# Three reorderings in a two-layer decoder trunk: a mean ahead of its root, sines behind two casts, and one store in place of two

## The chip, the cores and the metric

The kernel runs on 1 core of one Trainium2 chip. The metric is the device time of one execution in microseconds (us); the median of three runs stands for a kernel. TensorE (PE) multiplies matrices and loads weights (PEld), VectorE (DVE), ScalarE (ACT) and GpSimd (POOL) do the elementwise work, SyncE (SP) issues most of the DMAs.

## The reference

256 tokens of 1024 features pass through two layers. All is float32.

```
h = rmsnorm(x, norm_mix);  cb, cc, cu, q, k, v, g, ga, gb = split(h @ w_in)
y_conv = (cb * short_conv(cc * cu)) @ w_conv_out
q, k = rotary(q), rotary(k)              # sines and cosines of positions * frequencies
o = retention(q, k, v)                   # 4 heads, decay masks, two chunks of 128
o = (o - mean) * rsqrt(var + EPS) * ret_norm;   y_ret = (silu(g) * o) @ w_ret_out
x = x + (sigmoid(ga) * y_conv + sigmoid(gb) * y_ret) @ w_o
x = x + square(relu(rmsnorm(x, norm_mlp) @ w_up)) @ w_down
```

After the second layer the output is `rmsnorm(x, norm_final)`.

## The kernel before

The residual stream lies in SBUF with features on partitions and tokens along the free dimension. Weights come from HBM in 152 blocks of 1 MB, each as two half-blocks of 512 KB. For precision each half-block is split into a high and a low part: ACT casts it (`split`, L105), DVE subtracts the high part (L106). TensorE works on the parts, some 24 or 32 matmuls a block.

One call of `window` is one block. It writes out, in a fixed order, what each engine's queue gets: work at phase -1, then phase 0, the split of the first half of the block after next, phase 1, the split of the second half, phase 2, and the matmuls of its own block. Blocks 4 and 5 take the first split ahead of phase 0. `at(n, fn, ph=p)` puts a function into the window n blocks on; `products_at` does it for small matmuls. The schedule is manual: each engine runs its queue in this order and waits where a semaphore tells it to.

`rsqrt_begin` (L244) starts a reciprocal square root: ACT looks up a first value y (L246), DVE makes the mean m (L247); both read the same sums v in PSUM. `newton` then refines y: a square on ACT (L240), two multiplies on DVE (L241, L242). `rsqrt_begin` is called in `factors_begin` (once a layer, for the first norm, with Newton steps in the next two windows) and in `head_roots` (twice a layer, for the variances of two heads each, with Newton steps two and three windows on). Between `head_roots` and what follows on ACT's queue stand the collect of a projection (`collect`, L234 on ACT, L235 on DVE) and the two casts.

In layer 0 POOL reduces the rotary angles; `sines` (L389) takes two sines and an absolute value on ACT; `rotation_tables` (L395) makes the two tables with four POOL instructions; `rotations` (L422) multiplies the tables by the norm's factor on DVE, in window 8. ACT must load a table of functions (ACT_TABLE_LOAD) before it can take a sine, a root or a tanh.

At the end the last block's products are squared and summed for each of two halves of 128 tokens; `root(1)` gives the factor r. The last 512 features of the second half are scaled on DVE by `scaled` (L813) in two pieces of 256, each stored by a DMA that SP issues; the first 512 are scaled on ACT and stored from ACT's queue.

Of the kernel before, what the change touches and what calls it, by code (L numbers as in the profile page):

```python
# [16 lines left out]
ALU = mybir.AluOpType  # L17
# [8 lines left out]
EPS = 1e-6  # L26
# [27 lines left out]
def trunk_kernel(ctx, tc, px, pos, w, mask, gf, out):  # L54
    nc = tc.nc
# [31 lines left out]
    class Parts:  # L87
# [5 lines left out]
        def at(self, k):  # L93
            return self.tiles[k // (KT // 2)][:, k % (KT // 2)]
# [148 lines left out]

    def rsqrt_begin(y, m, v, scale):  # L244

        nc.scalar.activation(y, v, AF.Abs_reciprocal_sqrt, scale=scale, bias=eps)  # L246
        nc.vector.tensor_scalar(out=m, in0=v, scalar1=scale, scalar2=EPS, op0=ALU.mult, op1=ALU.add)  # L247

    def column_sums(o, hi, lo):

# [87 lines left out]
    for n in range(2):  # L338
        c = slice(4 * n, 4 * n + 4)
# [9 lines left out]
    def first_parts(norm=norm):  # L349

        def parts(i, *ks):
            for n, k in enumerate(ks):
                norm.split(k)
                split_half(i, n)

        at(0, parts, 1, 2, 3)
        at(1, parts, 2, 4, 5)
        at(2, parts, 3, 6, 7)
        at(3, norm.split, 0)
        for i, half in ((4, 0), (4, 1)):  # L360
            at(3, split_half, i, half)
        for p in range(NPAIR):
            at(3 if p < 3 else 4, norm.square, p)
        at(4, norm.fold)
        at(5, norm.split_sum)
# [37 lines left out]
    for layer in range(DEPTH):  # L403
# [4 lines left out]
        def factors_begin(norm=norm):  # L408
            rs_m, rs_a = (tmp.tile([P, T], F32, tag="tmp1", bufs=7, name=n) for n in ("rs_m", "rs_a"))
            rsqrt_begin(rr, rs_m, norm.total_ps, 1.0 / D)  # L410
            at(1, newton, rr, rs_a, rs_m, ph=-1)
            at(2, factors_end, rs_m, rs_a, ph=-1)
# [17 lines left out]
        if layer == 0:  # L430
            first_parts()
            at(0, reduce_angles)
            at(5, sines, ph=2)
            at(6, rotation_tables)
            at(9, nc.sync.dma_start, mask_sb, mask)
        if layer == 0:
            products_at(5, norm_total)
# [144 lines left out]
        def head_roots(i, st):  # L582

            if i == 0:
                new("rm", s8.tile([P, 2, HEADS, T], F32, tag="s8", name="rm"))
            rm = kept["rm"]
            h = slice(2 * i, 2 * i + 2)
            rs = rm[:, 0, h, :]
            rsqrt_begin(rs, rm[:, 1, h, :], st, 1.0 / T)
            later = 2 + i  # L590
            for n in range(2):
                at(later + n, lambda: newton(rs, t2("rs_a"), rm[:, 1, h, :]))
            for n in range(2):
                at(later + 1 + n, head_out, 2 * i + n, rs[:, n, :])
# [17 lines left out]
        for name, _ in IN_ORDER:  # L612
            n = seen[name] = seen.get(name, -1) + 1
# [183 lines left out]
    def root(j):  # L797

        rest, part = sums[j][:, 0:1], sums[j][:, 1:2]
        m, r, a = (small.tile([P, 1], F32, tag=f"{n}{j}", bufs=1, name=n) for n in ("fin_m", "fin_r", "fin_a"))  # L800
        nc.scalar.activation(r, part, AF.Sqrt, bias=rest)
        nc.vector.tensor_tensor(out=m, in0=part, in1=rest, op=ALU.add)
        nc.vector.reciprocal(r, r)
        nc.vector.scalar_tensor_tensor(out=a, in0=r, scalar=m, in1=r, op0=ALU.mult, op1=ALU.mult)
        nc.vector.scalar_tensor_tensor(out=r, in0=a, scalar=3.0, in1=r, op0=ALU.subtract, op1=ALU.mult)
        return r
# [6 lines left out]
    def scaled(j, n, c, r):  # L813

        f = slice(512 * n + c.start, 512 * n + c.stop)
        nc.vector.scalar_tensor_tensor(
            out=o[j][:, f], in0=ps[j][n][:, c], scalar=r, in1=gain[:, f], op0=ALU.mult, op1=ALU.mult
        )
        nc.sync.dma_start(out=out[tok[j], f], in_=o[j][:, f])
# [19 lines left out]
    c = HALVES[0]  # L839
# [2 lines left out]
    nc.vector.tensor_tensor(out=o[1][:, c], in0=ps[1][0], in1=gain[:, c], op=ALU.mult)  # L842
    squares(1, 1)
    r = root(1)
    for n in range(2):
        scaled(1, 1, slice(256 * n, 256 * n + 256), r)
    nc.scalar.activation(o[1][:, c], o[1][:, c], AF.Copy, scale=r)
    nc.scalar.dma_start(out=out[tok[1], c], in_=o[1][:, c])

# [73 lines left out]
```

## Time and profile before

| | |
|---|---|
| median of 3 runs | 876.67 us (876.5 to 876.76) |
| the profiled execution | 876.84 us |
| its span in the profile | 875.0 us |
| PE busy | 866.8 us (99%) |
| DVE, ACT, POOL busy | 680.2, 529.5, 308.4 us |
| mean granted TensorE clock | 0.999 of full speed |

The span runs from the first to the last instruction that the profiler recorded; the execution's own time has a little more around it. Busy TensorE time is modelled from pipelined matmuls, so that a short starvation shows better in the waits than in the busy share.

### The profile page before, as it was taken

Reading aid. Unit: us, or ns where it says so; the run is one execution under the profiler, and the core shown is the slowest. Engines: PE = TensorE matmul, PEld = TensorE weight load, DVE = VectorE, ACT = ScalarE, POOL = GpSimd, SP = SyncE. Lnnn points to the kernel's source line nnn. Section 1 sums busy time; section 2 is a strip of 40 time slices with the busy share of each in tenths; the row PEclk is TensorE's granted clock in tenths of the full one; section 3 lists DMA queues with packets and bytes.
Section 4 is the critical chain, followed back from the end, with each engine's and each line's share of the span. In section 5 each row is a group of like instructions: output and inputs, shape, how many; then the busy total and the mean of one; then the engine's idle time right before and its main releaser. Section 6 shows DMA issues by size and latency. Waiting matters only on the chain.

```text
span 875.0 us, 12663 instructions
## 1 busy us (share of the span) xinstructions
PE 866.8 (99%) x4846; PEld 754.1 (86%) x4846; DVE 680.2 (78%) x739; ACT 529.5 (61%) x761; POOL 308.4 (35%) x191
## 2 busy tenths in 40 slices
PE   9999999999999999999999999999999999999997
PEld 6888888888888888888888888888888888888885
DVE  5799899999898766555567989999979896663443
ACT  6766665956467777444447665578645587772333
POOL 3857755361213222000013587455411322240000
PEclk9999999999999999999999999999999999999999
DMA  9746455556655655555554555545565565565541
GB/s 329 231 170 208 138 194 183 168 174 226 202 194 170 216 187 193 196 188 187 178 199 167 183 172 195 171 158 187 185 210 175 194 198 189 191 218 171 196 137 48
DMA packets 45996, 163.53 MB, mean 187 GB/s; under 512 B 5104, under 2 KB 5744, under 8 KB 45936
## 3 DMA queue, kind: packets, MB, share of 16 engines
q1 hardware_dynamic: 45648, 162.29, 55.4%
q8 instruction: 38, 0.62, 0.3%
q10 hardware_dynamic: 288, 0.44, 0.2%
q14 instruction: 22, 0.18, 0.1%
HBM read 161.66 MB, written 1.05 MB: 186 GB/s over the span
## 4 chain that ended last, share of the span: by engine, by line
PE 87%; POOL 5%; DVE 4%; DMA 1%; ACT 1%; issue 1%; SPq 0%; DVEq 0%; POOLq 0%
PE ps L181 85%; DVE parts L106 2%; PE o_ps L181 1%; DMA pos_i<-pos 1%; POOL red L371 1%; POOL ang L386 1%; DMA raw<-w 1%; POOL mix_sum L281 1%; POOL rot L458 1%; POOL qk L459 0%; DVE sum L235 0%; PE sc_ps L181 0%; ACT parts L105 0%; POOL qk L451 0%; POOL acc L534 0%
## 5 line engine op out<-in xcount | busy, mean ns | idle before, releaser
L106 DVE TENSOR_TENSOR parts<-raw,parts 128x1024 fp32r<-128x1024 f32 (+1 forms) x304 | 436.7, 1474 | 94.2 <-ACT parts L105 93.8
L105 ACT CAST parts<-raw 128x1024 fp32r<-128x1024 f32 (+1 forms) x304 | 304.5, 1049 | 110.8 <-PE ps L181 79.8
L181 PE MATMUL ps<-mix,parts 128*128 128x512 f32 (+1 forms) x1792 | 316.1, 337 | 1.0 <-DVE parts L106 1.0
L181 PEld LDWEIGHTS ps<-mix,parts 128*128 128x128 f32 x1792 | 274.0, 188 | 38.9 <-DVE parts L106 1.6
L181 PE MATMUL ps<-mlp,parts 128*128 128x512 f32 (+1 forms) x1024 | 178.1, 336 | 0.0
L181 PEld LDWEIGHTS ps<-mlp,parts 128*128 128x128 f32 x1024 | 156.5, 188 | 20.9
L730 POOL TENSOR_TENSOR u<-u,rr2m 128x512 f32<-128x512 f32 x32 | 46.5, 1454 | 126.2 <-ACT u L729 113.1
L235 DVE TENSOR_TENSOR sum<-ps,sum 128x512 f32<-128x512 f32 x78 | 53.3, 684 | 47.4 <-ACT sum L234 47.3
L181 PE MATMUL ps<-up,parts 128*128 128x512 f32 (+1 forms) x512 | 88.9, 336 | 0.0
L181 PE MATMUL ps<-parts,up 128*128 128x512 f32 x384 | 87.5, 389 | 0.0
L181 PEld LDWEIGHTS ps<-up,parts 128*128 128x128 f32 x512 | 78.3, 188 | 10.5
L181 PEld LDWEIGHTS ps<-parts,up 128*128 128x128 f32 x384 | 71.9, 188 | 14.9
L234 ACT COPY sum<-ps 128x512 f32<-128x512 f32 x78 | 45.4, 583 | 61.9 <-PE ps L181 61.7
L181 PE MATMUL ps<-yr,parts 128*128 128x512 f32 (+1 forms) x256 | 44.7, 336 | 0.0
L181 PE MATMUL ps<-mg,parts 128*128 128x512 f32 (+1 forms) x256 | 44.7, 336 | 0.0
L181 PE MATMUL ps<-yc,parts 128*128 128x512 f32 (+1 forms) x256 | 44.7, 336 | 0.0
L181 PEld LDWEIGHTS ps<-yc,parts 128*128 128x128 f32 x256 | 39.1, 188 | 5.2
L181 PEld LDWEIGHTS ps<-yr,parts 128*128 128x128 f32 x256 | 39.1, 188 | 5.2
L181 PEld LDWEIGHTS ps<-mg,parts 128*128 128x128 f32 x256 | 39.1, 188 | 5.2
L181 PE MATMUL ps<-parts,mix 128*128 128x512 f32 x180 | 41.6, 392 | 0.0
L181 PEld LDWEIGHTS ps<-parts,mix 128*128 128x128 f32 x180 | 33.7, 188 | 7.5 <-ACT parts L105 0.6
L281 POOL TENSOR_TENSOR mix_sum<-mix_sum,sq 128x512 f32<-128x512 f32 x6 | 9.9, 1644 | 83.4 <-ACT sq L279 83.2
(166 smaller groups left out, 747.5 us busy)
## 6 DMA issues: line engine op xcount, KB each, us to landing
raw<-w SPq DMA_DIRECT2D x302, 512.0 KB, 4.0
raw<-w SPq DMA_DIRECT2D x4, 256.0 KB, 5.0
px_sb<-px SPq DMA_DIRECT2D x3, 256.0 KB, 7.3
mask_sb<-mask SPq DMA_DIRECT2D x1, 512.0 KB, 7.6
gain<-gf SPq DMA_DIRECT2D x1, 512.0 KB, 4.5
out<-o SPq DMA_DIRECT2D x2, 256.0 KB, 2.1
out<-o SPq DMA_DIRECT2D x2, 128.0 KB, 2.0
out<-o ACTq DMA_DIRECT2D x1, 256.0 KB, 2.2
```

The lines of the kernel that those rows point to most:

```text
L105: nc.scalar.copy(hi, src)
L106: nc.vector.tensor_tensor(out=lo, in0=src, in1=hi.bitcast(F32), op=ALU.subtract)
L181: nc.tensor.matmul(o, lhsT=a, rhs=b, start=start, stop=stop, skip_group_check=True)
L234: nc.scalar.copy(t, ps[:, :, 1, :])
L235: nc.vector.tensor_tensor(out=t, in0=ps[:, :, 0, :], in1=t, op=ALU.add)
L281: nc.gpsimd.tensor_tensor(out=self.sum, in0=self.sum, in1=sq, op=ALU.add)
L371: nc.gpsimd.tensor_scalar(out=out, in0=x_, scalar1=c0, op0=ALU.mult, **ops)
L386: nc.gpsimd.tensor_tensor(out=ang, in0=ang, in1=red, op=ALU.subtract)
L458: nc.gpsimd.tensor_tensor(out=w_, in0=w_, in1=both(sinr), op=ALU.mult)
L730: nc.gpsimd.tensor_tensor(out=u, in0=u, in1=both(rr2), op=ALU.mult)
```

## The change

In `rsqrt_begin` DVE's mean is issued ahead of ACT's root. The sines move from window 5 to window 6, still in phase 2, behind the casts of that window; the root of the first norm, in phase -1 of window 6, now stands ahead of them. The rotation tables move from window 6 to window 7. The last 512 features of the second half are scaled in one instruction and stored with one DMA.

```
     def rsqrt_begin(y, m, v, scale):

+        nc.vector.tensor_scalar(out=m, in0=v, scalar1=scale, scalar2=EPS, op0=ALU.mult, op1=ALU.add)
         nc.scalar.activation(y, v, AF.Abs_reciprocal_sqrt, scale=scale, bias=eps)
-        nc.vector.tensor_scalar(out=m, in0=v, scalar1=scale, scalar2=EPS, op0=ALU.mult, op1=ALU.add)
...
             at(0, reduce_angles)
-            at(5, sines, ph=2)
-            at(6, rotation_tables)
+            at(6, sines, ph=2)
+            at(7, rotation_tables)
...
     r = root(1)
-    for n in range(2):
-        scaled(1, 1, slice(256 * n, 256 * n + 256), r)
+    scaled(1, 1, c, r)
     nc.scalar.activation(o[1][:, c], o[1][:, c], AF.Copy, scale=r)
```

Here `c` is the slice of the first 512 columns of a half.

## Rows read from the trace of the kernel before

**Rows 1.** Chain that ended last, from 820 us: start us, us, what.
```profile
819.96 49.20 PE ps L181 x217
...
870.88 0.48 DVE o L816
```

**Rows 2.** Waits of PEld, 90 to 112 us: us in total, times, longest.
```profile
PEld ps L181 <- DVE parts L106: 1.6, 2, 1.0
```

**Rows 3.** Timeline of ACT, front: start us, us, instruction, idle before.
```profile
39.99 1.28 ACT L391 ACT_TABLE_LOAD   x1
...
42.57 1.28 ACT L246 ACT_TABLE_LOAD   x1
43.87 0.47 ACT L246 ACTIVATE rr<-mix_st,eps 128x256 f32<-128x256 f32 x1
...
45.51 2.00 ACT L105 CAST parts<-raw 128x1024 fp32r<-128x1024 f32 x2
47.41 0.41 ACT L240 ACTIVATE rs_a<-rr 128x256 f32<-128x256 f32 x1
```

**Rows 4.** Timeline of DVE, front.
```profile
40.01 1.23 DVE L106 TENSOR_TENSOR parts<-raw,parts 128x1024 fp32r<-128x1024 f32 x1 [0.21 <-ACT parts L105]
44.38 0.42 DVE L247 TENSOR_SCALAR rs_m<-mix_st 128x256 f32<-128x256 f32 x1 [3.14 <-ACT rr L246]
...
49.09 0.41 DVE L241 SCALAR_TENSOR_TENSOR rs_a<-rs_a,rs_m 128x256 f32<-128x256 f32 x1
...
57.67 1.52 DVE L424 TENSOR_TENSOR sinr<-sin_t,rr 128x256 f32<-128x256 f32 x1
```

**Rows 5.** Timeline of POOL, front: first rotation table, and what follows the fourth instruction.
```profile
42.64 0.74 POOL L397 TENSOR_TENSOR sin_t<-sh,turns 128x256 f32<-128x256 f32 x1 [3.26 <-ACT turns L393]
...
45.51 3.03 POOL L482 TENSOR_SCALAR v<-vt,mu 128x256 f32<-128x256 f32 x2
```

**Rows 6.** Timeline of ACT around the heads' roots, layer 0.
```profile
158.05 0.69 ACT L246 ACTIVATE rm<-var_ps,eps 128x512 f32<-128x512 f32 x1
...
159.10 2.01 ACT L105 CAST parts<-raw 128x1024 fp32r<-128x1024 f32 x2
...
168.09 0.69 ACT L246 ACTIVATE rm<-var_ps,eps 128x512 f32<-128x512 f32 x1
...
169.15 2.01 ACT L105 CAST parts<-raw 128x1024 fp32r<-128x1024 f32 x2
```

**Rows 7.** Timeline of DVE around the heads' roots, layer 0.
```profile
159.06 0.68 DVE L247 TENSOR_SCALAR rm<-var_ps 128x512 f32<-128x512 f32 x1
...
160.26 3.45 DVE L106 TENSOR_TENSOR parts<-raw,parts 128x1024 fp32r<-128x1024 f32 x2
...
164.82 3.43 DVE L106 TENSOR_TENSOR parts<-raw,parts 128x1024 fp32r<-128x1024 f32 x2 [0.17 <-ACT parts L105]
...
169.49 0.69 DVE L247 TENSOR_SCALAR rm<-var_ps 128x512 f32<-128x512 f32 x1
...
170.69 3.45 DVE L106 TENSOR_TENSOR parts<-raw,parts 128x1024 fp32r<-128x1024 f32 x2
```

**Rows 8.** Timeline of PE, two output projections of four blocks each, layer 0.
```profile
192.97 22.35 PE L181 MATMUL ps<-yc,parts 128*128 128x512 f32 x128
215.16 22.35 PE L181 MATMUL ps<-yr,parts 128*128 128x512 f32 x128
```

**Rows 9.** Timeline of DVE, cut after one half-block.
```profile
199.98 1.21 DVE L106 TENSOR_TENSOR parts<-raw,parts 128x1024 fp32r<-128x1024 f32 x1
```

**Rows 10.** Timeline of DVE, the same block's split in layer 1.
```profile
627.13 3.44 DVE L106 TENSOR_TENSOR parts<-raw,parts 128x1024 fp32r<-128x1024 f32 x2
```

**Rows 11.** Timeline of PE, the second output projection in layer 1.
```profile
644.93 22.35 PE L181 MATMUL ps<-yr,parts 128*128 128x512 f32 x128
```

**Rows 12.** Timeline of the end, the two 512-wide scalings of the first token half.
```profile
866.09 1.41 DVE L816 SCALAR_TENSOR_TENSOR o<-ps,fin_r,gain 128x512 f32<-128x512 f32 x2
```

**Rows 13.** Timeline of SP from 871 us: the last two stores' issues.
```profile
871.39 0.81 SPq L819 DMA_DIRECT2D out<-o  x2
```

## Prediction, made before the change was run

> **What bounds the kernel now.** I read the chain that ended last first: its late part is one unbroken run of matmuls, and only the last 6 us belong to the other engines [rows 1]. So the span is TensorE's queue plus a short tail, and an edit elsewhere counts where it makes TensorE start a block later or earlier, or where it changes that tail. Next I looked for places where TensorE starves. The weight loads' waits give two, 1.6 us together, both for the low half of a weight block that DVE makes at L106 [rows 2]. They lie near 95 and 107 us, in layer 0. DVE is behind there, and the chain that holds it back can be followed to the front part: DVE waits there for the convolution's tap on ACT, which waited for POOL's product, which waited for a DVE sum. Nothing in that chain waits for TensorE, so I take a DVE that is late or early at 49 us to be late or early by as much at 95 us. That makes the front's price easy: each us of DVE time there is a us of TensorE time, a gain of at most the 1.6 us that is lost now.
>
> **Part 1, the front (mean ahead of root, sines behind the casts).** Today the queue of ACT loads the sine table at 39.99, the root's table at 42.57, starts the root at 43.87, the casts of the next block at 45.51 and Newton's square at 47.41 [rows 3]. DVE ended a split at 41.24 (40.01 + 1.23) and then sat 3.14 us until the root had ended, though the mean reads only the same sums; I read this as an order kept between two readers of one PSUM bank, in program order [rows 4]. After the change the mean can start at 41.24 and end at 41.66. The root's table loads at 39.99 and is there at 41.27, so now ACT waits: the root starts at 41.70 (0.04 for the signal, as between the root's end at 44.34 and the mean at 44.38). From root to casts is 1.64 us (43.87 to 45.51), so casts at 43.34; from casts to the next instruction 1.90 (45.51 to 47.41), so the sines' table at 45.24; the sines with their load take 2.58 (39.99 to 42.57), so Newton's square starts at 47.82, 0.41 later than now. The number of table loads stays the same if every set holds squares.
>
> DVE has by then only the work behind the two casts and is through with it near 46.7 (second cast done at 45.34, a split of 1.23 behind it). So of the 3.14 us that it was given, it hands most back at once: Newton's multiply waits for the square, which ends about 48.23, and starts at 48.27 instead of 49.09 [rows 4]. What is left of the gain is 0.82 us.
>
> Against that stands the moved POOL work. The four rotation-table instructions take 2.87 us (42.64 to 45.51) and ran while DVE mostly idled [rows 5]; now they start near 47.9, beside Newton's two multiplies and the next splits. The nearest price is the rotations at L424: 1.52 us against 0.41 for Newton's multiply of the same 256 columns [rows 4], so some 1.1 us for each of two DVE instructions under POOL's long products. As those two fill 3 us, DVE loses up to 0.7 of the time in which POOL multiplies two tensors. Of the tables about half is such work, the rest takes a single tensor. At 0.7 for half of 2.87 that is 1.0; at 0.7 for all, 2.0; with no clash, 0. I take 0.9, as the collect between reads PSUM. DVE is then 0.1 us late at 49 us where it was to be 0.8 early. **Front: +0.1 us, between -0.8 and +1.2.**
>
> The Trainium skill, page SBUF — State Buffer, section "SBUF: two separate sides", says that a DVE instruction with two SBUF inputs and a GpSimd one that reads SBUF exclude each other for a whole instruction. By that, single-tensor GpSimd work would cost as much as products, and the sum would take the +1.2 end; the lengthened L424 agrees with an exclusion, and no row shown here prices the single-tensor kind.
>
> **Part 2, the roots of the retention heads.** The same function serves four more places: two per layer. Here the order matters the other way. In layer 0 ACT's first root ran from 158.05 [rows 6], and DVE came to its mean only at 159.06, ending 159.74 [rows 7], without having waited for ACT. DVE was busy, not held. With the order reversed ACT must wait: root at 159.78, 1.73 late. Queued behind it on ACT are a collect and two casts, 159.10 becoming 160.83; the first cast (half of 2.01) is done at 161.84 and DVE's split, waiting for it, starts at 161.9 instead of 160.26. In the next block the split at 164.82 already waited 0.17 for its cast, so it follows ACT's 1.73: 166.55. DVE is full from there to the second mean, 169.49 becoming 171.22, ending 171.91. The second root then starts at 171.95 instead of 168.09, 3.86 late; the casts at 173.01 instead of 169.15; the split at 174.06 instead of 170.69. **DVE is 3.4 us late**, and it has no idle time until past 204 to get it back.
>
> Who waits? The tightest block after that is the third of the convolution's output projection. TensorE runs those four blocks from 192.97 and the next four from 215.16, 5.55 us each, so the third starts at 204.07 [rows 8]. Its first half-block is split by 201.19 [rows 9]: 2.88 us to spare. With 3.37 off, TensorE waits 0.49. **Roots in layer 0: +0.5 us.** Bounds: 0, if the wait doesn't arise or is made good, and 1.5, if both waits grow by half a us, since beyond 2.88 each us of lateness is paid in full. In layer 1 the pattern is the same, but its block starts 11.1 us ahead of 644.93, at 633.83, and its first half is split near 628.3 (half of the pair begun at 627.13, the quicker one) [rows 10, 11]: 5.5 us to spare, so 3.4 costs nothing. Layer 1's norm is cheap as well, since its margins are as wide.
>
> **Part 3, the store.** The last 512 features are now scaled in one instruction and stored with one DMA. The first 256-wide piece took 0.48 from 870.88 [rows 1] and SP issued at 871.39, both issues done at 872.20 [rows 13]. A 512-wide piece takes 0.70 (1.41 for two) [rows 12], so its issue starts at 871.61, 0.22 later than the first does now, and ends, with one issue of half of 0.81, at 872.0, 0.2 earlier than the last does now. ACT's own store leaves at about the same moment with as many bytes. If the bytes decide, the start counts: +0.2; if the last descriptor decides, -0.2. I take +0.1.
>
> **Sum.** 0.1 + 0.5 + 0.1 = +0.7 us. The profiled execution took 876.84 (span 875.0, 1.84 around it), so 877.5; it lies 0.17 above the median, so 877.4 for the median. Against 0.2% (1.75 us, about what a measurement of this kernel tells from no change) that is the same.
>
> **Rivals.** (a) Forecast, 0.50: 877.4, its own range 876.8 to 878.1. (b) The roots' wait costs nothing, because ACT isn't held or DVE makes it good before 204 us; for it speaks that no reader-waits-for-reader is seen at these roots today, against it the 3.14 us in the front. 876.7 + 0.2 = 876.9, 0.25. (c) POOL's tables don't clash with Newton and DVE keeps its 0.8, without the roots' cost: 876.67 - 0.8 + 0.1 = 876.0; if more of the 3.14 survives, up to 1.6 and a tail of -0.2: 874.9. For it: the 3.14 idle is real; against: the square behind the sines. 0.10, of which 0.03 is past 0.2%. (d) Slower: the two root waits are longer than I find, as POOL's gate products fall differently on DVE's splits. Place: the block at 204.07. It decides when DVE is over 4.4 us late (1.5 there, with 0.2 elsewhere): at 4.9 the sum is 2.0 + 0.2, so 878.9; 0.08, of which 0.06 is slower. (e) Slower: ACT has to load a table again for Newton's square, which now follows the sines with no root between. Price: one load of 1.28 (39.99 to 41.27) ahead of the square, which DVE and TensorE pay: 877.4 + 1.3 = 878.7; 0.04, of which 0.03 is slower. Against it: casts and the square ran after the root's load with no new one [rows 3]. The Trainium skill, page ScalarE: Activation LUTs, section "Table sets: the hidden batching unit", names relu, copy, identity and abs as in every set and doesn't name the square; no run here shows a square behind the sines yet. (f) Slower: all four table instructions hold DVE off, not only the products: front +1.2, so 878.5; 0.03, of which 0.02 is slower. That is the rule of the page SBUF — State Buffer above.
>
> So faster 0.03, slower 0.11, same 0.86. The range 876.0 to 878.5 leaves out the far part of (c), most of (d) and (e) and half of (f).
>
> **What would show it.** Front: mean near 41.3, root near 41.7, sines' table near 45.2, square near 47.8, Newton's multiply near 48.3 and lengthened beside POOL's tables; the two waits near 95 and 107 still about 1.6 us. Roots: ACT idle ahead of its roots until the mean's end, some 1.7 and 2.1 us, DVE's splits 3.4 late, a new wait of TensorE near 204 in layer 0 and none in layer 1. Tail: one SP issue near 0.2 later after the root. Wrong would be: no wait of ACT at the roots, five loads in the first 60 us, or waits near 95 that are gone.

## The result, and the profile after

The changed kernel takes 882.85 us (median of 5, 879.99 to 883.31) against 876.67 (5, 876.5 to 877.27): a ratio of 1.0059, 95% interval 1.0045 to 1.0072. It is slower by some 5 to 6 us, and none of the predicted cases held that. The profiled execution took 882.85 us, 6.01 more than that of before.

The place shows in TensorE's queue. First the timeline of PE in the kernel before, 145 to 460 us; one row groups matmuls that follow each other without a gap:

```profile
164.77 0.62 PE L181 MATMUL var_ps<-osq,ones 128*128 128x512 f32 x2
165.23 27.91 PE L181 MATMUL ps<-mix,parts 128*128 128x512 f32 x160
...
270.86 77.82 PE L181 MATMUL ps<-mlp,parts 128*128 128x512 f32 x448
348.51 88.91 PE L181 MATMUL ps<-up,parts 128*128 128x512 f32 x512
437.26 21.96 PE L181 MATMUL ps<-parts,mix 128*128 128x512 f32 x96
```

The same view of the changed kernel:

```profile
164.30 0.39 PE L181 MATMUL var_ps<-osq,ones 128*128 128x512 f32 x1
165.25 0.50 PE L181 MATMUL var_ps<-osq,ones 128*128 128x512 f32 x1 [0.56 <-DVE osq L106]
165.58 28.42 PE L181 MATMUL ps<-mix,parts 128*128 128x512 f32 x160
193.84 22.79 PE L181 MATMUL ps<-yc,parts 128*128 128x512 f32 x128
...
273.23 79.31 PE L181 MATMUL ps<-mlp,parts 128*128 128x512 f32 x448
352.38 90.61 PE L181 MATMUL ps<-up,parts 128*128 128x512 f32 x512
442.82 17.42 PE L181 MATMUL ps<-parts,mix 128*128 128x512 f32 x76
```

Three things are to be seen. At 164.30 TensorE comes to the column sums of the heads' squares (`osq`, for the variances of heads 2 and 3) 0.47 us ahead of before. The second of the two sums then waits for DVE: the block behind them starts at 165.58 instead of 165.23, so that 0.82 us are lost there. From that wait on the same matmuls take longer: 512 of them 90.61 instead of 88.91 us, 128 of them 22.79 instead of 22.35 [rows 8], with no wait among them. Start to start, a block of 32 steps by 5.65 instead of 5.55 us (22.62 against 22.19 for four). This goes on for 49 blocks, 27 to 75, up to the value projection of layer 1, where other shapes of matmul come: 277.24 us from 165.58 to 442.82, where before took 272.03. That is 5.21 us without one visible stall.

The granted clock doesn't explain it. The windows view, 280 to 430 us, of before (us, then busy time of each engine with its count of instructions, granted clock, DMA share, GB/s):

```profile
280.00:430.00 150.00, 150.00 (x868) 132.25 (x867) 95.09 (x103) 88.23 (x119) 24.22 (x17) 1.00 0.57 193
```

and of the changed kernel:

```profile
280.00:430.00 150.00, 150.00 (x851) 130.11 (x851) 93.37 (x102) 87.88 (x119) 24.43 (x18) 1.00 0.56 189
```

Both are granted 1.00, the upper level of 2.4 GHz, and PE counts as busy throughout; only the number of matmuls in 150 us falls, 868 to 851. What DMA carries falls in the same proportion, 193 to 189 GB/s.

The wait's origin is DVE's queue. Its timeline in the kernel before has the low half of those squares at

```profile
163.63 0.41 DVE L106 TENSOR_TENSOR osq<-osq 128x256 fp32r<-128x256 f32 x1
```

so it ended at 164.04, 0.73 us ahead of the pair of sums at 164.77, whose second one reads it. The changed kernel's timeline of DVE:

```profile
158.59 0.68 DVE L246 TENSOR_SCALAR rm<-var_ps 128x512 f32<-128x512 f32 x1
160.50 0.69 DVE L235 TENSOR_TENSOR ta<-ps,ta 128x512 f32<-128x512 f32 x1 [1.23 <-ACT ta L234]
161.45 3.41 DVE L106 TENSOR_TENSOR parts<-raw,parts 128x1024 fp32r<-128x1024 f32 x2 [0.26 <-ACT parts L105]
164.78 0.41 DVE L106 TENSOR_TENSOR osq<-osq 128x256 fp32r<-128x256 f32 x1
...
173.49 3.33 DVE L106 TENSOR_TENSOR parts<-raw,parts 128x1024 fp32r<-128x1024 f32 x2 [0.26 <-ACT parts L105]
```

and ACT's:

```profile
159.31 0.69 ACT L247 ACTIVATE rm<-var_ps,eps 128x512 f32<-128x512 f32 x1 [1.74 <-DVE rm L246]
...
171.35 0.69 ACT L247 ACTIVATE rm<-var_ps,eps 128x512 f32<-128x512 f32 x1 [2.02 <-DVE rm L246]
```

ACT's root waits 1.74 us for DVE's mean, as forecast; ACT's collect and casts come later; DVE idles 1.23 + 0.26 for them; and `osq` ends at 165.19 instead of 164.04, while TensorE is there 0.47 sooner. Layer 1 stays free of cost: the projection at 644.93 [rows 11] now starts at 650.48, 5.55 us later, no more than the 5.56 by which the value projection was already late.

So 6.01 = -0.47 + 0.82 + 5.21 + 0.47 (rounding leaves 0.02). The last term is the tail's: the last scalings start at 876.42 instead of 870.88 [rows 1], 5.54 later, and what is left of 6.01 falls behind that.

### The profile page after: what moved, and what is told of

The parts are those of the page before. It is cut to its first block, busy times and chain, and to the rows that moved or that the text cites. A ratio compares the mean times of both kernels' runs of the same rounds, so it can differ in the third digit from the quotient of the medians.

```text
span 881.1 us, 12653 instructions
## 1 busy us (share of the span) xinstructions
PE 872.8 (99%) x4846; PEld 755.0 (86%) x4846; DVE 680.1 (77%) x738; ACT 529.3 (60%) x761; POOL 303.9 (34%) x191
## 4 chain that ended last, share of the span: by engine, by line
PE 81%; DVE 9%; POOL 5%; issue 2%; ACT 2%; DMA 1%; SPq 0%; DVEq 0%; POOLq 0%
PE ps L181 79%; DVE parts L106 5%; DMA pos_i<-pos 1%; DVE sum L235 1%; POOL mix_sum L281 1%; ACT parts L105 1%; PE o_ps L181 1%; POOL ang L386 1%; POOL rot L458 1%; POOL red L371 1%; POOL qk L459 0%; POOL sg L496 0%; DMA px_sb<-px 0%; DVE acc L523 0%; DVE acc L526 0%
## 5 line engine op out<-in xcount | busy, mean ns | idle before, releaser
L181 PE MATMUL ps<-mlp,parts 128*128 128x512 f32 (+1 forms) x1024 | 179.9, 338 | 0.0
L281 POOL TENSOR_TENSOR mix_sum<-mix_sum,sq 128x512 f32<-128x512 f32 x6 | 11.7, 1955 | 85.1 <-ACT sq L279 84.9
```

What stands on the lines that cost most here:

```text
L181: nc.tensor.matmul(o, lhsT=a, rhs=b, start=start, stop=stop, skip_group_check=True)
L281: nc.gpsimd.tensor_tensor(out=self.sum, in0=self.sum, in1=sq, op=ALU.add)
```

## Experiments

Run beside the experiments, the kernel before gave medians of 876.94 to 877.14 us, chip by chip; each comparison below is with the runs on its own chip, in brackets the number of runs. "The switch" is an argument `mean_first` of `rsqrt_begin` that chooses the order for each caller:

```
+    def rsqrt_begin(y, m, v, scale, mean_first=False):
+        if mean_first:
             nc.vector.tensor_scalar(out=m, in0=v, ...)
         nc.scalar.activation(y, v, AF.Abs_reciprocal_sqrt, ...)
+        if not mean_first:
             nc.vector.tensor_scalar(out=m, in0=v, ...)
```

**The changed kernel with the heads' roots put back.** Only the first norm keeps the mean ahead.

```
-            rsqrt_begin(rr, rs_m, norm.total_ps, 1.0 / D)
+            rsqrt_begin(rr, rs_m, norm.total_ps, 1.0 / D, True)
```

> The changed kernel with the root ahead of the mean again at the four calls for the retention heads; front and store as changed. Theory (a starved TensorE falls into a slower step): without ACT's two waits near 159 and 171 us DVE's low half of the last head's squares is in time, TensorE does not wait at 164.3, and the 49 blocks after it take 5.55 us each and not 5.65: 876.67 - 0.47 (front) + 0.5 (end) = 876.7 us. Rival 1 (the longer blocks come with the moved sines, tables or the changed front): only the wait of 0.8 us goes, about 882 us, blocks still 5.65. Rival 2 (the longer blocks come and go with executions, whatever the kernel): times spread between 877 and 883.

877.47 us (11 runs) against 877.01 (27): ratio 1.0007, 0.9998 to 1.0016. The loss is gone; the sums don't wait, and the blocks step by 5.55 us.

**The heads' roots alone**, in the kernel before:

```
-            rsqrt_begin(rs, rm[:, 1, h, :], st, 1.0 / T)
+            rsqrt_begin(rs, rm[:, 1, h, :], st, 1.0 / T, True)
```

> The kernel before with the mean ahead of the root at the four calls for the retention heads alone. Theory (a starved TensorE falls into a slower step): ACT waits about 1.7 and 2.0 us ahead of its roots, TensorE waits about 0.8 us for the low half of the last head's squares near 165 us, and blocks then take 5.65 us until 442 us: 876.67 + 0.8 + 5.2 = 882.7 us, single executions between 879 and 884. Rival 1 (longer blocks come with the front): 877.5 us, blocks 5.55. Rival 2: spread without order.

882.26 us (5 runs), ratio 1.0059, 1.0046 to 1.0072: all of the loss. ACT waits 1.74 and 2.03 us, the blocks step by 5.65 us from 27 to 75, and the timeline of PE has the same wait:

```profile
165.80 0.50 PE L181 MATMUL var_ps<-osq,ones 128*128 128x512 f32 x1 [0.25 <-DVE osq L106]
```

**The front alone** (the switch for the first norm; sines and tables moved) and **the store alone**, both in the kernel before:

> The kernel before with the mean ahead of the root for the two norms, and sines and tables one window later; heads and store as before. Theory: DVE 0.45 us early from 49 us on, the two waits near 95 and 107 us shorter by as much, nothing else: 876.2 us, blocks 5.55 throughout. Rival 1: blocks of 5.65 from 165 us, about 881.5 us. The forecast on record had +0.1 us for the front, 876.8.

876.84 us (11), ratio 0.9998, 0.9989 to 1.0007.

> The kernel before with the last 512 features scaled in one instruction and stored with one DMA. From the two traces the stretch from the factor to the last instruction is 0.48 us longer: 877.15 us. The forecast on record had +0.1, 876.8. If the longer end is only the slower state of that execution: 876.7.

877.58 us (11), ratio 1.0007, 0.9998 to 1.0016. Neither can be told from no change. Against 877.01 the three parts alone give +5.25, -0.17 and +0.57: 5.65 together, beside 6.18 between the medians of the two kernels.

**One pair of heads at a time.** Each layer has two roots, for heads 0 and 1 and for heads 2 and 3. The squares that come late lie behind the first root, so the first should carry the loss.

```
+            rsqrt_begin(rs, rm[:, 1, h, :], st, 1.0 / T, i == 0)     # or i == 1
```

> The kernel before with the mean ahead of the root for heads 0 and 1 alone, in both layers; heads 2 and 3 keep the root first. Theory (a starved TensorE falls into a slower step, and the starving comes from the first of the two waits): ACT waits 1.7 us once, DVE's low half of the last head's squares is 1.7 us late near 165 us, TensorE waits 0.6 to 0.9 us there, then blocks of 5.65 us until 442 us: 882.5 us. Rival (the lateness of 3.4 us by both waits does it, at the tightest block near 204 us): 877 us.

879.76 us (7 runs, 879.21 to 882.98) against 876.94 (22), ratio 1.0045, 1.003 to 1.0059.

> The kernel before with the mean ahead of the root for heads 2 and 3 alone, in both layers. Theory: ACT waits about 2 us near 170 us, but the column sums of the last head were already under way, no wait of TensorE before 204 us and 1.7 us of lateness against 2.9 to spare there, so blocks of 5.55 throughout: 877.0 us, as before. Rival: 882 us.

876.95 us (10), ratio 1.0000, 0.9991 to 1.001, although ACT waits its 2.1 us there. So the loss hangs on the first pair, though at the median it alone costs 2.8 us and both pairs 5.3. The first pair's runs lie apart, five between 879.2 and 881.0 and two near 882.9, and the profiled one (879.76) shows one way for this in its timeline of PE; the other six have no trace:

```profile
194.41 22.77 PE L181 MATMUL ps<-yc,parts 128*128 128x512 f32 x128
...
273.55 0.28 PE L181 MATMUL mlp_st<-mlp_sh,ones 128*128 128x256 f32 x1
...
273.79 77.82 PE L181 MATMUL ps<-mlp,parts 128*128 128x512 f32 x448
351.45 88.91 PE L181 MATMUL ps<-up,parts 128*128 128x512 f32 x512
```

Here the longer step ends at the two small sums for the second norm, near 273.6; from there the times are those of before to the hundredth. In the changed kernel it ran past the same two sums. The waits for `osq` were unlike in length too: 0.3 us of the weight loads here, 0.6 with both pairs, 0.9 in the changed kernel.

**Keeping the root's wait and taking away TensorE's.** The heads' means go first, and the column sums of heads 2 and 3, with the root that reads them, come one block later:

```
-                products_at(4, head_sums, 1)
+                products_at(5, head_sums, 1)
```

> The kernel before with the mean ahead of the root for all heads, and the column sums of heads 2 and 3 handed to TensorE one block later (all that follows from them moves one block as well). Theory: ACT still waits ahead of its roots, but DVE's low half of the squares is ready when TensorE comes to it, so no wait near 165 us and blocks of 5.55 us: 877 us, plus at most some 0.5 us for the tight blocks near 200 us; if a wait there again starts the slower step, 4 us more. Rival (the order of ACT and DVE itself, not TensorE's wait, makes the matmuls slower): blocks of 5.65, 882 us.

877.22 us (10), ratio 0.9998, 0.9989 to 1.0007. ACT still waits (1.74 and 1.08 us), DVE's splits still come late, but the timeline of PE is back at the old step:

```profile
170.04 0.62 PE L181 MATMUL var_ps<-osq,ones 128*128 128x512 f32 x2
...
192.71 22.35 PE L181 MATMUL ps<-yc,parts 128*128 128x512 f32 x128
```

So neither the late splits nor ACT's wait costs anything that can be measured; TensorE's stop at the sums does, and what follows it.

**What holds the longer step.** The heads' change was kept, and products of a matrix of ones were added between regular blocks, in five sizes. They stand behind the wait and change nothing ahead of it.

```
+    def extra(count, n):
...
+        for _ in range(count):
+            mm(ps[:, :n], ones, ones[:, None, :].broadcast_to([P, n // P, P]), True, True)
+    for n, count, cols in ((29, 1, 128), (32, 2, 256), (35, 1, 512), (38, 4, 512), (41, 12, 512)):
+        products_at(n, extra, count, cols)
```

> The kernel before with the mean ahead of the root for all heads (882.3 us), and small extra products of ones by ones behind five blocks of layer 0: one of 128 columns behind block 29, two of 256 behind 32, one of 512 behind 35, four of 512 behind 38, twelve of 512 behind 41; their results are not read. Theory (the slower step is a state of TensorE's queue that another sequence of matmuls can end): blocks of 5.65 from 165 us on until one of these, 5.55 behind it; what the products take is about 0.1, 0.3, 0.2, 0.9 and 2.6 us. Rival (something outside TensorE, as DVE, ACT or the transfers beside it, sets the pace): 5.65 on to 442 us whatever is put in between.

882.53 us (one run). Its timeline of PE:

```profile
166.05 0.50 PE L181 MATMUL var_ps<-osq,ones 128*128 128x512 f32 x1 [0.57 <-DVE osq L106]
166.39 16.81 PE L181 MATMUL ps<-mix,parts 128*128 128x512 f32 x96
...
216.66 0.39 PE L181 MATMUL extra<-ones 128*128 128x512 f32 x1
216.89 17.12 PE L181 MATMUL ps<-yr,parts 128*128 128x512 f32 x96
233.85 1.09 PE L181 MATMUL extra<-ones 128*128 128x512 f32 x4
234.77 5.71 PE L181 MATMUL ps<-yr,parts 128*128 128x512 f32 x32
```

This wait of 0.57 us, as long as the changed kernel's 0.56, is followed by the shorter step (16.81 for 96 matmuls). The longer one (17.12) begins behind a single product at 216.66, where nothing waits, and ends behind four. So the step isn't a lasting effect of the wait alone; in this run it changed twice where the regular order of matmuls was broken and nothing waited.

**Four products behind block 27**, in the kernel with all heads' means first, to see if they bring the step back:

```
+    products_at(27, extra, 4, 512)
```

> The kernel before with the mean ahead of the root for all heads (882.3 us), and four small products of ones by ones of 512 columns behind block 27, the first whole block after TensorE's wait; their results are not read. Theory (an irregular stretch of matmuls draws the step anew, and this one ended the slower step behind block 38): blocks of 5.65 end with block 27, later ones take 5.55; 1.0 us more work, 0.8 us of waiting, 5 us less of slow blocks: 877 + 0.8 + 1.0 = 878.8 us. Rival (the slower step is kept by what runs beside TensorE): 882.3 + 1.0 = 883.3 us.

878.77 us (11 runs), ratio 1.0025, 1.0014 to 1.0036. Nine runs lie between 878.35 and 878.95, the size of the wait and of the four products (0.92 us, from 233.85 to 234.77 above). Two lie at 883.51 and 884.0. The profile is of the latter: there the wait (0.3 us of the weight loads) is followed by a block of the shorter step, 5.55 us from start to start, and the four products by the longer one (22.79 for 128). That the nine had the shorter step behind the four products is read from their times; they have no trace. On that reading the same place gives the one or the other from run to run.

**Waits without a late DVE, and the same products without a wait.** Both start from the kernel before. In the one a product of ones is copied by ACT one to three times and multiplied again, so that TensorE waits; in the other both products are of ones.

```
+    def trip(copies):
...
+        mm(ps[:, :P], ones, ones, True, True)
+        nc.scalar.copy(echo, ps[:, :P])          # left out in the other kernel
+        for _ in range(copies - 1):              # left out
+            nc.scalar.copy(echo, echo.bitcast(F32))
+        mm(ps[:, P:2 * P], ones, echo, True, True)    # ones for echo in the other
+    for n, copies in ((47, 1), (50, 2), (53, 3), (56, 1), (59, 2), (62, 3), (65, 1), (68, 2), (71, 3)):
+        products_at(n, trip, copies)
```

> The kernel before with nine made waits of TensorE in layer 0's MLP, behind every third block from 47 to 71: a product of ones by ones (128 columns), one, two or three copies of it on ACT, and a product of that copy, so that TensorE waits some 0.5 to 1.5 us each time; nothing reads the results. Theory (any wait can leave TensorE in the slower step): behind some of the nine the next three blocks take 5.65 us, behind the others 5.55, 0.3 us more for each stretch. Rival (only the late column sum at 165 us does it): 5.55 behind all nine.

888.63 us (one run). Seven of the nine waits are followed by the shorter step (16.86 for 96, 22.41 for the last 128), two by the longer one:

```profile
354.47 0.33 PE L181 MATMUL trip<-echo,ones 128*128 128x128 f32 x1 [0.68 <-ACT echo L411]
354.64 16.86 PE L181 MATMUL ps<-up,parts 128*128 128x512 f32 x96
...
372.57 0.33 PE L181 MATMUL trip<-echo,ones 128*128 128x128 f32 x1 [1.01 <-ACT echo L411]
372.73 17.18 PE L181 MATMUL ps<-up,parts 128*128 128x512 f32 x96
```

> The kernel before with the same two products behind the same nine blocks, the second also of ones by ones, so that TensorE has nothing to wait for. Theory in its first form (a wait is needed): 5.55 behind all nine, 0.1 to 0.3 us more for each pair of products. Theory in its wider form (any break in the regular sequence can do it, as one product of 512 columns behind block 35 did): some stretches of 5.65.

881.78 us (one run). All nine stretches have the longer step, with no wait anywhere:

```profile
281.90 0.34 PE L181 MATMUL trip<-ones 128*128 128x128 f32 x2
282.08 17.17 PE L181 MATMUL ps<-mlp,parts 128*128 128x512 f32 x96
...
419.56 22.82 PE L181 MATMUL ps<-up,parts 128*128 128x512 f32 x128
```

A wait is therefore neither needed for the longer step nor sure to bring it. In this kernel the other engines' instructions and their order are those of before, so a changed order on another engine isn't needed either.

**The whole change with the sums one block later**, the edit to `products_at` above:

> The changed kernel, whole, with the column sums of heads 2 and 3 handed to TensorE one block later. Theory: all that the change lost in the middle hangs on TensorE's one wait near 165 us and the slower step behind it, so what is left is the front's gain of about 0.3 and the end's loss of about 0.5: 877.2 us beside 877.0 before, blocks of 5.55 us from 165 us on, and no single execution above 878.5. Rival (the changed order of ACT and DVE at the heads costs more than that wait): 879 us or more.

877.04 us (11) against 877.14 (15): ratio 1.0001, 0.9992 to 1.001. Its timeline of PE:

```profile
169.78 0.62 PE L181 MATMUL var_ps<-osq,ones 128*128 128x512 f32 x2
...
347.98 88.91 PE L181 MATMUL ps<-up,parts 128*128 128x512 f32 x512
```

One line takes back the loss of the whole change. Nothing here beats the kernel before by what can be measured.

## Why the prediction was wrong

**The front: right, and worth nothing.** Timeline of ACT in the changed kernel:

```profile
41.27 0.47 ACT L247 ACTIVATE rr<-mix_st,eps 128x256 f32<-128x256 f32 x1 [0.33 <-DVE rs_m L246]
...
44.93 1.28 ACT L391 ACT_TABLE_LOAD   x1
...
47.40 0.40 ACT L240 ACTIVATE rs_a<-rr 128x256 f32<-128x256 f32 x1
```

and of DVE:

```profile
40.82 0.42 DVE L246 TENSOR_SCALAR rs_m<-mix_st 128x256 f32<-128x256 f32 x1
...
47.84 0.76 DVE L241 SCALAR_TENSOR_TENSOR rs_a<-rs_a,rs_m 128x256 f32<-128x256 f32 x1 [1.48 <-ACT rs_a L240]
48.63 0.58 DVE L242 SCALAR_TENSOR_TENSOR rr<-rs_a,rr 128x256 f32<-128x256 f32 x1
...
49.74 2.66 DVE L106 TENSOR_TENSOR parts<-raw,parts 128x1024 fp32r<-128x1024 f32 x2
52.32 0.41 DVE L241 SCALAR_TENSOR_TENSOR rs_a<-rs_a,rs_m 128x256 f32<-128x256 f32 x1
```

Each step of part 1 is there, some 0.4 us earlier than forecast, because this execution was that much ahead when DVE was free for the mean: 40.82, where before DVE's split ended at 41.24 [rows 4]. Counted from that moment, Newton's multiply starts after 7.02 us instead of 7.85, the forecast gain of 0.82. The two multiplies are then longer by 0.35 and 0.16, and the split behind them, beside POOL's last table instruction, by 0.31 (2.66 against 2.35 us in the kernel before): 0.82 where 0.9 was taken. The second multiply ran beside POOL's single-tensor work (0.98 us from 48.41), so rival (f)'s mechanism exists in part. The Trainium skill, page SBUF — State Buffer, section "SBUF: two separate sides", has a DVE instruction with two SBUF inputs and a GpSimd one that reads SBUF exclude each other for a whole instruction; the trace shows less, as the multiply was through at 49.21 and POOL's instruction lasted to 49.39. So the gain and the price cancel: the next Newton step (52.32) starts 11.50 us after that moment, exactly as before (52.74, from the timeline of DVE in the kernel before). No fifth table load came in the first 60 us, so (e) is out. TensorE's waits of 90 to 112 us were 1.0 instead of 1.6 [rows 2], but in the other runs they were 0.5 to 1.5 with the new order and 0.6 to 1.6 with the old, so the 0.47 us by which TensorE is ahead at 164 is not put down to the change.

**The roots' waits: right; who pays for them: wrong.** ACT's waits (1.74 and 2.02 against 1.73 and 2.1) and DVE's lateness hold: the split at 170.69 [rows 7] comes at 173.49, and with the 0.47 added 3.27 late where 3.4 was forecast. The step that failed is "Who waits?". It looked at weight blocks only, found the tightest at 204.07 with 2.88 us to spare, and put 0.5 us there. No wait arose there, and TensorE's own loss has a part in this: its third block came 1.08 us later than before, at 205.15, and DVE's split for it 2.65 us later, at 202.63, so that 1.3 us were left. But TensorE also reads what DVE makes of the heads themselves, and the low half of `osq`, behind the split of 160.26, was ready only 0.73 us ahead of the pair of sums at 164.77. That reader stood in no part of the sum and in no rival.

**A wait counted at its own length: wrong, and the larger error.** Each term, and rival (d), took a microsecond of TensorE's wait for a microsecond of time. The wait that arose was 0.82 us, inside the range by itself (876.84 - 0.47 + 0.82 + 0.47 = 877.7). The 5.21 us that took the result out of it are the longer step of the next 49 blocks, and the rows that the prediction read [rows 8, 11] are all of the shorter step. But the longer step isn't the change's own, and the profile of before held it too, at other places. Two rows of 64 matmuls of equal shapes from its timeline of PE, the first at the longer step and the second at the shorter:

```profile
27.56 11.45 PE L181 MATMUL ps<-mix,parts 128*128 128x512 f32 x64
...
153.66 11.27 PE L181 MATMUL ps<-mix,parts 128*128 128x512 f32 x64
```

The same 64 matmuls of layer 0 could also have either step from one execution to another. First the kernel before, then the store alone, which issues the same work up to the last scalings:

```profile
126.07 11.34 PE L181 MATMUL ps<-mix,parts 128*128 128x512 f32 x64
```

```profile
126.92 11.54 PE L181 MATMUL ps<-mix,parts 128*128 128x512 f32 x64
```

So a comparison of equal rows within the one trace would have shown that there are two steps, though not that a stop at 164 us would bring on the longer one.

**The store: right in sign.** The forecast +0.1 (±0.2) came out at +0.47 in the profile, beyond its bounds. The last scaling takes 0.75 us from 876.42, and its store is issued at 877.20, beside ACT's at 877.17; the timeline of both queues:

```profile
877.17 0.38 ACTq L847 DMA_DIRECT2D out<-o  x1
...
877.20 0.33 SPq L819 DMA_DIRECT2D out<-o  x1
```

Its start is later than the first of the old two would be (870.88 to 871.39 is 0.51 [rows 1, 13], now 0.78), and ACT's store, of the same size as before, now takes 2.9 us from issue to landing (median of the page's DMA issues) instead of 2.2. That the two stores, leaving together, hold each other up is read from this, not tried. Alone the edit gave +0.57 (interval of the ratio 0.9998 to 1.0016), which agrees and isn't told from nothing.

**What stays open.** Shown: the loss comes from the first pair's order through the late `osq`, and a break in TensorE's regular sequence can leave either of two steps behind it, which can then last for as long as the matmuls stay alike. Not shown: what at the break decides. The wait's length doesn't (0.57 us was followed by the one in one kernel, 0.56 by the other in another), nor the place of the break (by the times, nine of eleven against two in one kernel).

## What to carry to other kernels

When an engine is made later, list every reader of what it makes, not only the largest stream: here 256 columns of squares, ready 0.73 us ahead of the sums, counted for more than weights with 2.88. Where TensorE's queue is the span, compare the time of equal rows of matmuls, within one trace and between the two, before looking for waits; a step of 5.65 instead of 5.55 us hides in a busy share of 99%. And give a small product a block of slack where its reader allows it: moving the sums one block took back all of a loss of 5 us.

## What the runs showed of the hardware that was not expected

The same sequence of matmuls ran at two steps, both at a granted clock of 1.00: 5.55 or 5.65 us for 32 matmuls of the weight blocks (88.91 or 90.61 us for 512). These matmuls have 512 and 256 columns in turn, and the starts of the single ones near 300 us show the longer step as a rhythm of its own: in the kernel before the gaps are 230 and 117 ns throughout, in the changed kernel they repeat after six, 241, 120, 236, 113, 233 and 117 ns, so that six take 1060 ns instead of 1040. A wait, or a few products of another shape, can switch it either way, and the kernel before shows both too; the longer one persisted for up to 49 blocks, 5.21 us in all. With only two 128-column products between the blocks, nine of nine stretches took the longer step; with a wait between those two products, two of nine.
